# Attention scores from operands stacked on the contraction rows: three matmuls per head and block in place of five

## The chip, the cores and the metric

The kernel runs on one core of one Trainium2 chip. A core has TensorE (PE in the rows; its weight loads are shown as PEld), VectorE (DVE), ScalarE (ACT), GpSimd (POOL) and SyncE (SP, which here only starts DMAs). The metric is device microseconds (us) from start to end of one execution, lower is better. All products are made in an fp32 form (fp32r) with each operand split into a high part, rounded to fp32r, and a low part, the rest; a product is then three matmuls (high by high, low by high, high by low).

## What is computed

Two blocks in a row on 512 tokens of width 1024: the first has attention with a forget gate, a short convolution, a gated merge and a mixture of experts; the second has retention, a Fourier branch and a feed-forward part. The change lies in the attention of the first block alone. Cut to that:

```python
q = rms_norm(q.reshape(b, s, 8, 64), q_norm_g[i])
k = rms_norm(k.reshape(b, s, 8, 64), k_norm_g[i])
log_f = jax.nn.log_sigmoid(f_logit + b_f[i])
...
c = jnp.cumsum(log_f, axis=1).transpose(0, 2, 1)
...
    logits = jnp.einsum('bhqd,bhkd->bhqk', qb, kh) * scale
    logits = logits + (cqb[..., :, None] - c[..., None, :])
    logits = jnp.where(causal, logits, NEG_INF)
    probs = jax.nn.softmax(logits, axis=-1)
    return jnp.einsum('bhqk,bhkd->bhqd', probs, vh)
```

There are 8 heads of 64 features; queries are taken in four blocks of 128, and block qb looks at (qb + 1) * 128 keys.

## The kernel before

The program is one long unrolled list. A scheduler puts each engine's instructions in a fixed order at build time; on the chip each engine runs its list in that order and waits where an operand or a buffer is not there yet. Tiles come from pools by size: `B` tiles (128 x 512 fp32, 35 buffers), `T` tiles (128 x 1024, 5 buffers), and PSUM pools `mm` (4 banks), `sd` (2 banks, for scores and head outputs) and `tp` (2 banks, for transposes; `ptr` takes one).

The stages around the change, in order of time:

- `gemm_q`, `gemm_k`, `gemm_v` project the tokens, one 512-wide block each (`tok_gemm`: 24 matmuls of 512 columns for each weight piece of 256 rows). Each weight piece is cast to its high part `whi` on ACT (L187) and its low part `wlo` is made on DVE (L188). For q and k, `qk_evac` copies each token tile out (`qn`), squares it on ACT, sums on DVE, takes the root on POOL and scales on DVE.
- `forget_gate` is woven into `gemm_k`. It ends with the cumulative sum `csum` (8 heads on 8 partitions), its two parts, and the negated parts. Before the change these go by eight DMAs into four tiles `cq`, `ck`, in which head h owns four partitions: rows (c high, c low, 1, 1) for the queries and (1, 1, -c high, -c low) for the keys.
- `decays` makes 16 exponentials on ACT (`dm_f`, `dm_b`, L647) and three products on DVE (L649, L650) for the second block. It needs two `T` tiles; where it falls in the engines' order is up to the scheduler.
- `qk_turn(hp)` transposes a pair of heads (8 PE transposes into two `tp` banks) and takes them out: one ACT instruction for the high part and one DVE instruction for the low part, for q and for k, each over both heads' 128 partitions. `attention_start` calls it for all four pairs while `gemm_v` runs.
- `attention` runs `values(h)` for the 8 heads, woven with the convolution's projections (`ps_cc`, `ps_cu`, `ps_cb`) and then an output projection (`ps_f`), eight steps of six 512-column matmuls for each head. A head: ten transposes of the probabilities (`pt_p`, from the `tp` banks), `scores(h + 1, (0, 1))`, twelve matmuls with v (`ps_y`), `scores(h + 1, (2, 3))`.
- `scores` makes one block with five matmuls into one `sd` bank: three on the head's 64 rows (L204, L205, L206 inside `mm3`), one on the four gate rows (L851), one bf16 matmul that adds the causal mask on the diagonal (L852). Behind it: maximum on DVE (L854), exponential on ACT (L857), reciprocal and scaling on DVE.

Of the kernel before, what the change touches and what calls it, by code (L numbers as in the profile page):

```python
# [94 lines left out]
def weave(main, side, ratio, drain=True, acc=0.0):  # L95
    """Steps of `main`, with `ratio` steps of `side` traced after each."""
    for _ in main:
        acc += ratio
        while side is not None and acc >= 1.0:
            acc -= 1.0  # L100
            next(side, 0)
        yield 1
    if side is not None and drain:
        yield from side
# [12 lines left out]
class Feed:  # L117
    """Jobs in the order in which their results are used, traced ahead of the use."""
# [4 lines left out]
    def plan(self, jobs):  # L123
        """Queue jobs; the numbers by which to take their results."""
# [15 lines left out]
def fused_blocks(ctx, tc, a, out, probe=None, upto=99):  # L140
# [61 lines left out]
    def mm3(ps, x, y, first, last):  # L202
        """ps (+)= x.T @ y, each operand a (hi, lo) pair."""
# [19 lines left out]
    def tok_gemm(acts, pieces, ktn, evac, nt=NT, last=0, pre=None):  # L223
        """One 512-wide block of acts @ w, tokens on partitions.
        pieces: (offset, width, rows(kt, n)) of the block's columns.
        last: weight pieces at the end that each token tile takes in one go."""
# [41 lines left out]
    def feat_plan(pieces):  # L268
        """[128, 8, 256] of weights as two splits; pieces: (k offset, n, col offset, width, rows)."""
# [11 lines left out]
    def feat_step(nos, acts, name):  # L281
        """The next 128 features of a plan, features on partitions."""
# [5 lines left out]
    def feat4(w, evac, acts):  # L288
        """acts @ w for a w of 512 rows, features on partitions."""
# [27 lines left out]
    def gate_merge(wcols, bias, acts, first, second, dst):  # L317
        """dst = sigmoid(h @ w_a + b_a) * first + sigmoid(h @ w_b + b_b) * second, split."""
# [65 lines left out]
    def sq_sum(x, ss=None):  # L384
        """Sum over the columns given of squares / D."""
# [6 lines left out]
    def first_half(which):  # L392
        """Takes the squares of rows' first halves, for a norm of the whole ones later."""
# [7 lines left out]
    class NormT:  # L401
        """RMS norm of token rows, transposed and split: feature k on partitions."""

        def __init__(self, gain=None, keep=None, over=None, cols=None, on_act=(), on_dve=()):
            """gain: a row on all partitions; or cols: (gain, shift or None) by feature on partitions.
            keep: where the rows go, whose transposes are then kept for the last tile only."""
# [11 lines left out]
        def behind(self, t, x, part, ins, then=None):  # L418
            """do(), with tile t - 1 turned only now, behind ins."""
# [79 lines left out]
    # q, k: per-head norm; v: split  # L499
# [28 lines left out]
    # rows (c, 1) of the queries and (1, -c) of the keys, in high and low parts, c the cumulative  # L528
    # forget gate; head h on partitions 32 (h % 4) + (0 .. 3) of tile h // 4
    cq = [B("cq", F32R), B("cq", F32R)]  # L530
    ck = [B("ck", F32R), B("ck", F32R)]
    for u in cq + ck:
        act.copy(u, bc(one, [P, 512]))
# [11 lines left out]
    # columns of small parameters, by transposing rows of 128  # L545
# [109 lines left out]
    # md rows: shift1, gain1, g1, shift2, gain2, g2, ctx shift, ctx gain  # L655
# [20 lines left out]
    def md_cols(name, gain, shift):  # L676
        """Two of md's rows as columns, features on partitions."""
# [118 lines left out]
    def forget_gate():  # L796
        """Cumulative log sigmoid of the forget gate."""
# [14 lines left out]
        ch, cl, nh, nl = (B("c_" + s, F32R) for s in ("hi", "lo", "nhi", "nlo"))  # L812
        split(csum[:8, :], ch[:8, :], cl[:8, :])
# [92 lines left out]
    def attention():  # L906
        for h in range(8):
            yield from values(h)
# [924 lines left out]
```

## Time and profile before

| | |
|---|---|
| Time, median of three runs | 1509.5 us (1504.53 to 1510.33) |
| The profiled execution: span from first to last instruction | 1516.9 us |
| TensorE busy | 1470.2 us, 97% of the span |
| VectorE, ScalarE busy | 978.6 us, 717.6 us |
| Granted TensorE clock, mean over the span | 0.985 of full speed |
| Chain that ended last, TensorE's share of the span | 51% |

The profiled execution has no time of its own besides its span; the span alone is 7.4 us (0.5%) above the median of the three runs without a profile. A group of instructions is read as: line, engine, operation, output<-inputs, how often, busy time, mean duration. Durations of matmuls overlap, since a matmul starts before the one ahead of it has left the array; what a matmul costs the engine is the distance from its start to the next start.

### The profile page before, as it was taken

To read this page: it belongs to the slowest core of one execution; us is meant where nothing else is said; L and a number is where in the kernel's file an instruction comes from. 1 tells how busy PE (TensorE), PEld (TensorE's weight loads), DVE (VectorE), ACT (ScalarE), POOL (GpSimd) and SP (SyncE) were. 2 spreads that over 40 slices of the span, in tenths; PEclk is the share of its full clock that TensorE was granted. 3 is DMA by queue.
4 is the path that set the end of the run, shared out by engine and by line. 5 is a ranking of instruction groups with operands and counts; after the bars stand their busy time and mean duration, and the time that the engine had idled before them with its cause. 6 is when DMAs were issued, how large, how long until landed. Compare 5 with 4: busy or idle time off the path is not lost.

```text
span 1516.9 us, 18405 instructions
## 1 busy us (share of the span) xinstructions
PE 1470.2 (97%) x6989; PEld 1183.3 (78%) x6989; DVE 978.6 (65%) x1573; ACT 717.6 (47%) x1172; POOL 106.1 (7%) x120
## 2 busy tenths in 40 slices
PE   7999999999999989899999999999999999999997
PEld 5777778887887657677888888888778888888886
DVE  6656464678689988555677777556855664366634
ACT  6643334333459878566444455343345443234432
POOL 2400000000122030311000000000000000000001
PEclk9999999999999999899999999999999999999999
DMA  6421113458489999622322212746623332433221
GB/s 219 123 63 56 56 56 122 159 178 284 149 259 309 369 357 374 217 84 83 105 69 77 67 60 83 238 154 213 218 82 87 108 95 86 112 90 105 80 73 56
DMA packets 174441, 218.99 MB, mean 144 GB/s; under 512 B 9280, under 2 KB 133708, under 8 KB 174348
## 3 DMA queue, kind: packets, MB, share of 16 engines
q1 hardware_dynamic: 169612, 200.98, 40.8%
q0 software_dynamic: 2944, 10.49, 2.2%
q10 hardware_dynamic: 1792, 6.29, 1.1%
q8 instruction: 57, 0.93, 0.3%
q14 instruction: 36, 0.29, 0.1%
HBM read 206.63 MB, written 11.04 MB: 144 GB/s over the span
## 4 chain that ended last, share of the span: by engine, by line
PE 51%; ACT 3%; DVE 2%; issue 1%; POOL 1%; POOLq 0%; ACTq 0%
PE ps_tok L206 6%; PE ps_tok L205 6%; PE ps_tok L204 6%; PE ps_up L204 5%; PE ps_up L205 5%; PE ps_up L206 5%; PE ps_gt L206 2%; PE ps_gt L205 2%; PE ps_gt L204 2%; PE ps_g L204 1%; PE ps_g L206 1%; PE ps_g L205 1%; PE ps_ro L204 1%; PE ps_ro L205 1%; PE ps_ro L206 1%
## 5 line engine op out<-in xcount | busy, mean ns | idle before, releaser
L188 DVE TENSOR_TENSOR wlo<-raw,whi 128x1024 fp32r<-128x1024 f32 x248 | 300.4, 1216 | 265.6 <-ACT whi L187 253.8
L187 ACT CAST whi<-raw 128x1024 fp32r<-128x1024 f32 x248 | 258.1, 1044 | 322.1 <-PE ps_tok L206 119.8
L204 PE MATMUL ps_up<-nt_hi,whi 128*128 128x512 f32 (+2 forms) x368 | 141.5, 385 | 2.8 <-ACT nt_hi L187 2.8
L205 PE MATMUL ps_up<-nt_lo,whi 128*128 128x512 f32 (+2 forms) x368 | 141.6, 385 | 0.0
L206 PE MATMUL ps_up<-nt_hi,wlo 128*128 128x512 f32 (+2 forms) x368 | 141.4, 384 | 0.0
L204 PE MATMUL ps_tok<-whi,nt_hi 128*128 128x512 f32 x288 | 115.3, 402 | 3.2 <-ACT nt_hi L187 3.2
L205 PE MATMUL ps_tok<-wlo,nt_hi 128*128 128x512 f32 x288 | 113.2, 395 | 0.0
L206 PE MATMUL ps_tok<-whi,nt_lo 128*128 128x512 f32 x288 | 112.8, 394 | 0.0
L204 PE MATMUL ps_gt<-nt_hi,whi 128*128 128x512 f32 x256 | 99.7, 389 | 0.0
L205 PE MATMUL ps_gt<-nt_lo,whi 128*128 128x512 f32 x256 | 99.7, 389 | 0.0
L206 PE MATMUL ps_gt<-nt_hi,wlo 128*128 128x512 f32 x256 | 99.7, 389 | 0.0
L204 PEld LDWEIGHTS ps_up<-nt_hi,whi 128*128 128x128 f32 x368 | 69.8, 190 | 16.0 <-ACT nt_hi L187 3.0
L711 DVE SCALAR_TENSOR_TENSOR mod_acc<-raw,silu_c,mod_acc 128x1024 f32<-128x1024 f32 x56 | 70.7, 1277 | 17.0 <-DMA raw<-in_w_mod_dram 16.6
L205 PEld LDWEIGHTS ps_up<-nt_lo,whi 128*128 128x128 f32 x368 | 69.7, 189 | 13.3 <-DVE nt_lo L188 0.2
L206 PEld LDWEIGHTS ps_up<-nt_hi,wlo 128*128 128x128 f32 x368 | 69.7, 189 | 13.1
L188 DVE TENSOR_TENSOR wlo<-raw_a,whi 128x1024 fp32r<-128x1024 f32 x56 | 67.9, 1231 | 3.3 <-ACT whi L187 3.3
L204 PE MATMUL ps_tok<-whi,hid_hi 128*128 128x512 f32 x176 | 68.6, 390 | 0.0
L205 PE MATMUL ps_tok<-wlo,hid_hi 128*128 128x512 f32 x176 | 68.5, 389 | 0.0
L206 PE MATMUL ps_tok<-whi,hid_lo 128*128 128x512 f32 x176 | 68.4, 390 | 0.0
L204 PEld LDWEIGHTS ps_tok<-whi,nt_hi 128*128 128x128 f32 x288 | 54.6, 190 | 15.1 <-ACT nt_hi L187 4.6
L187 ACT CAST whi<-raw_a 128x1024 fp32r<-128x1024 f32 x56 | 58.0, 1051 | 17.8 <-PE ps_tok L206 7.1
L206 PEld LDWEIGHTS ps_tok<-whi,nt_lo 128*128 128x128 f32 x288 | 54.4, 189 | 12.0 <-DVE nt_lo L188 0.9
(461 smaller groups left out, 3334.8 us busy)
## 6 DMA issues: line engine op xcount, KB each, us to landing
raw<-in_w_in_dram SPq DMA_DIRECT2D x31, 1024.0 KB
raw<-in_w_up_dram SPq DMA_DIRECT2D x55, 512.0 KB
raw<-in_w_mod_dram SPq DMA_DIRECT2D x24, 1024.0 KB
raw<-in_w_down_dram SPq DMA_DIRECT2D x15, 1024.0 KB
raw_a<-in_w_gate_dram SPq DMA_DIRECT2D x19, 512.0 KB
raw_a<-in_w_up_dram SPq DMA_DIRECT2D x19, 512.0 KB
raw_a<-in_w_down_dram SPq DMA_DIRECT2D x9, 1024.0 KB
raw<-in_w_branch_gate_dram SPq DMA_DIRECT2D x8, 1024.0 KB
```

Source lines behind the costliest of these rows:

```text
L187: act.copy(hi, src)
L188: return (eng or dve).tensor_tensor(lo, src, hi.bitcast(F32), op=ALU.subtract)
L204: pe.matmul(ps, x[0], y[0], start=first, stop=False)
L205: pe.matmul(ps, x[0], y[1], start=False, stop=False)
L206: pe.matmul(ps, x[1], y[0], start=False, stop=last)
L711: dve.scalar_tensor_tensor(ac, rv[:, j, :], col, ac, op0=ALU.mult, op1=ALU.add)
```

## The change

Each head gets four tiles of its own. `q_hl` holds the high part of q on 64 partitions and its low part on the other 64; `k_hh` holds the high part of k on both halves; `q_hc` holds the high part of q on partitions 0 to 63 and the head's four gate rows on 64 to 67; `k_lc` holds the low part of k and its four gate rows. A block of scores is then one matmul over 128 rows (high by high plus low by high), one over 68 rows (high by low plus the gate term) and the mask matmul as before. The gate rows go from SBUF to a DRAM tile `crows` by four SP DMAs and from there into rows 64 to 67 of each head's tiles by 16 DMAs that POOL issues. `qk_turn` takes a pair out with eight ACT and four DVE instructions of 64 partitions. Turns 0 and 1 stay in `attention_start`; turns 2 and 3 move into `attention`, ahead of `values(2)` and `values(4)`. The rest of the diff takes comments out, which shifts line numbers (the mask matmul L852 becomes L860).

```diff
-    cq = [B("cq", F32R), B("cq", F32R)]
-    ck = [B("ck", F32R), B("ck", F32R)]
-    for u in cq + ck:
-        act.copy(u, bc(one, [P, 512]))
+    crow = [T(n, F32R) for n in ("c_pos", "c_one", "c_neg")]
+    act.copy(crow[1][:8, :], bc(one[:8, :], [8, 1024]))
+    crows = drm.tile([2, 8, 4, S], F32, name="crows")
+    crows_dst = [[crows[0, :, 0:2]], [crows[0, :, 2:4], crows[1, :, 0:2]], [crows[1, :, 2:4]]]
...
-        ch, cl, nh, nl = (B("c_" + s, F32R) for s in ("hi", "lo", "nhi", "nlo"))
-        split(csum[:8, :], ch[:8, :], cl[:8, :])
-        act.mul(nh[:8, :], ch[:8, :].bitcast(F32), -1.0)
-        act.mul(nl[:8, :], cl[:8, :].bitcast(F32), -1.0)
-        for i in range(2):
-            for d, r, s in ((cq, 0, ch), (cq, 1, cl), (ck, 2, nh), (ck, 3, nl)):
-                sp.dma_start(d[i][r:r + 97:32, :].bitcast(F32), s[4 * i:4 * i + 4, :].bitcast(F32))
+        split(csum[:8, :], crow[0][:8, :512], crow[0][:8, 512:])
+        act.mul(crow[2][:8, :], crow[0][:8, :].bitcast(F32), -1.0)
+        for u, dsts in zip(crow, crows_dst):
+            for d in dsts:
+                sp.dma_start(d.rearrange("h i s -> h (i s)"), u[:8, :].bitcast(F32))
...
     def qk_turn(hp):
+        pts = []
         for w in range(2):
             pt = ptr("pt_qk")
             for t in range(NT):
                 pe.transpose(pt[:, t * P:(t + 1) * P], qk[w][t][:, hp * P:(hp + 1) * P], ident)
-            h, l = B("qkT_hi", F32R), B("qkT_lo", F32R)
-            act.activation(h, pt, AF.Copy, scale=gq[:, w:w + 1])
-            dve.scalar_tensor_tensor(l, pt, gq[:, w:w + 1], h.bitcast(F32), op0=ALU.mult, op1=ALU.subtract)
-            qkT[w].append((h, l))
+            pts.append(pt)
+        for j in range(2):
+            h = 2 * hp + j
+            r = slice(64 * j, 64 * j + 64)
+            o = slice(64 - 64 * j, 128 - 64 * j)
+            q, k = pts[0][r, :], pts[1][r, :]
+            g = [gq[r, w:w + 1] for w in range(2)]
+            qs, ks, q2, k2 = (B(n, F32R) for n in ("q_hl", "k_hh", "q_hc", "k_lc"))
+            act.activation(qs[r, :], q, AF.Copy, scale=g[0])
+            act.activation(ks[r, :], k, AF.Copy, scale=g[1])
+            dve.scalar_tensor_tensor(qs[o, :], q, g[0], qs[r, :].bitcast(F32), op0=ALU.mult, op1=ALU.subtract)
+            act.activation(q2[:64, :], q, AF.Copy, scale=g[0])
+            act.activation(ks[o, :], k, AF.Copy, scale=g[1])
+            dve.scalar_tensor_tensor(k2[:64, :], k, g[1], ks[r, :].bitcast(F32), op0=ALU.mult, op1=ALU.subtract)
+            for i, dst in enumerate((q2, k2)):
+                pool.dma_start(dst[64:68, :].bitcast(F32), crows[i, h])
+            head_ops[h] = qs, ks, q2, k2
...
-            mm3(ps[:, :nk], q, k, True, False)
-            pe.matmul(ps[:, :nk], cqh[:, qb * P:nk], ckh[:, :nk], start=False, stop=False)
+            pe.matmul(ps[:, :nk], qs[:, qb * P:nk], ks[:, :nk], start=True, stop=False)
+            pe.matmul(ps[:, :nk], q2[:68, qb * P:nk], k2[:68, :nk], start=False, stop=False)
             pe.matmul(ps[:, qb * P:nk], identb, maskb, start=False, stop=True)
...
     def attention_start():
-        for hp in range(4):
+        for hp in range(2):
             qk_turn(hp)
...
     def attention():
         for h in range(8):
+            if h in (2, 4):
+                qk_turn(h // 2 + 1)
             yield from values(h)
```

On PE, at the scores of a head's blocks 2 and 3 behind twelve projection matmuls, before the change:

```order
L204 MATMUL ps_s<-qkT_hi 128x384
L205 MATMUL ps_s<-qkT_lo,qkT_hi 128x384
L206 MATMUL ps_s<-qkT_hi,qkT_lo 128x384
L851 MATMUL ps_s<-ck,cq 128x384
L852 LDWEIGHTS identb
L852 MATMUL ps_s<-maskb,identb 128x128
L204 MATMUL ps_s<-qkT_hi 128x512
L205 MATMUL ps_s<-qkT_lo,qkT_hi 128x512
L206 MATMUL ps_s<-qkT_hi,qkT_lo 128x512
L851 MATMUL ps_s<-ck,cq 128x512
L852 LDWEIGHTS identb
L852 MATMUL ps_s<-maskb,identb 128x128
```

and in the changed kernel:

```order
L858 MATMUL ps_s<-k_hh,q_hl 128x384
L859 MATMUL ps_s<-k_lc,q_hc 128x384
L860 LDWEIGHTS identb
L860 MATMUL ps_s<-maskb,identb 128x128
L858 MATMUL ps_s<-k_hh,q_hl 128x512
L859 MATMUL ps_s<-k_lc,q_hc 128x512
L860 LDWEIGHTS identb
L860 MATMUL ps_s<-maskb,identb 128x128
```

Four matmuls are gone from each such pair of blocks; nothing else of PE's list moved between them.

On ACT, behind the forget gate, where `c_pos` (before: `c_hi`, `c_lo`) is the cumulative sum and `qn`, `sq` are the k tiles' copies and squares; before the change:

```order
L187 CAST c_hi<-csum 8x512
L187 CAST whi<-raw 128x1024
L814 ACTIVATE c_nhi<-c_hi 8x512
L815 ACTIVATE c_nlo<-c_lo 8x512
L505 COPY qn<-ps_tok 128x512
L506 ACTIVATE sq<-qn 128x512
L505 COPY qn<-ps_tok 128x512
L506 ACTIVATE sq<-qn 128x512
L505 COPY qn<-ps_tok 128x512
L506 ACTIVATE sq<-qn 128x512
L187 CAST whi<-raw 128x1024 x2
```

and in the changed kernel, from the negation on:

```order
L813 ACTIVATE c_neg<-c_pos 8x1024
L647 ACT_TABLE_LOAD
L647 ACTIVATE dm_f<-once,eneg 128x128
L505 COPY qn<-ps_tok 128x512
L647 ACTIVATE dm_f<-once,eneg 128x128
L506 ACTIVATE sq<-qn 128x512
L647 ACTIVATE dm_f<-once,eneg 128x128 x5
L505 COPY qn<-ps_tok 128x512
L647 ACTIVATE dm_f<-once,eneg 128x128
L506 ACTIVATE sq<-qn 128x512
L647 ACTIVATE dm_b<-once,eneg 128x128 x8
L505 COPY qn<-ps_tok 128x512
```

The sixteen exponentials of `decays`, which stood between the q tiles' copies ahead of the forget gate, now stand behind it, with the table load for the exponential ahead of them; on DVE their three products moved in the same way, to behind the forget gate's sum.

On ACT, between the scores of head 2 and the copies of its turned probabilities, before the change:

```order
L857 ACTIVATE pr,rs<-ps_s,nm 128x384
L857 ACTIVATE pr,rs<-ps_s,nm 128x512
L187 CAST whi<-raw 128x1024
L187 CAST p_hi<-pt_p 128x512 x2
L187 CAST p_hi<-pt_p 128x256
```

and in the changed kernel:

```order
L865 ACTIVATE pr,rs<-ps_s,nm 128x384
L865 ACTIVATE pr,rs<-ps_s,nm 128x512
L187 CAST whi<-raw 128x1024
L839 ACTIVATE q_hl<-pt_qk,gq 64x512
L840 ACTIVATE k_hh<-pt_qk,gq 64x512
L843 ACTIVATE k_hh<-pt_qk,gq 64x512
L842 ACTIVATE q_hc<-pt_qk,gq 64x512
L839 ACTIVATE q_hl<-pt_qk,gq 64x512
L840 ACTIVATE k_hh<-pt_qk,gq 64x512
L843 ACTIVATE k_hh<-pt_qk,gq 64x512
L842 ACTIVATE q_hc<-pt_qk,gq 64x512
L187 CAST p_hi<-pt_p 128x512 x2
```

The eight evictions of turn 2 stand there now, ahead of the copies `p_hi`. On PE at the same place the eight transposes of turn 2 are followed by twelve projection matmuls, blocks 0 and 1 of head 3's scores and seven more projection matmuls before the first `pt_p` of head 2, which before stood directly there.

## Rows read from the trace of the kernel before

**Rows 1.** The page, busy time of each engine, and granted clock in 40 slices.

```profile
PE 1470.2 (97%) x6989; PEld 1183.3 (78%) x6989; DVE 978.6 (65%) x1573; ACT 717.6 (47%) x1172; POOL 106.1 (7%) x120
...
PEclk9999999999999999899999999999999999999999
```

**Rows 2.** Windows of 25 us over the attention stage; busy us, then granted clock.

```profile
100.00:125.00 25.00, 25.00 (x122) 18.74 (x121) 12.97 (x29) 10.11 (x24) 0.00 (x0) 1.00 0.28 85
125.00:150.00 25.00, 25.00 (x116) 19.46 (x115) 16.34 (x31) 8.66 (x17) 0.00 (x0) 0.93 0.13 43
150.00:175.00 25.00, 25.00 (x109) 18.34 (x108) 11.68 (x24) 8.17 (x18) 0.00 (x0) 0.93 0.12 43
175.00:200.00 25.00, 25.00 (x109) 19.22 (x108) 13.03 (x27) 8.82 (x19) 0.00 (x0) 0.87 0.13 43
```

**Rows 3.** Timeline of PE, scores of blocks 2 and 3; start, duration.

```profile
171.26 0.39 PE L206 MATMUL ps_cc<-nt_hi,wlo 128*128 128x512 f32 x1
171.58 0.44 PE L204 MATMUL ps_s<-qkT_hi 64*128 64x384 f32 x1
171.86 0.33 PE L205 MATMUL ps_s<-qkT_lo,qkT_hi 64*128 64x384 f32 x1
172.03 0.34 PE L206 MATMUL ps_s<-qkT_hi,qkT_lo 64*128 64x384 f32 x1
172.29 0.43 PE L851 MATMUL ps_s<-ck,cq 4*128 4x384 f32 x1
172.66 0.23 PE L852 MATMUL ps_s<-maskb,identb 128*128 128x128 bf16 x1
172.81 0.50 PE L204 MATMUL ps_s<-qkT_hi 64*128 64x512 f32 x1
173.16 0.39 PE L205 MATMUL ps_s<-qkT_lo,qkT_hi 64*128 64x512 f32 x1
173.39 0.39 PE L206 MATMUL ps_s<-qkT_hi,qkT_lo 64*128 64x512 f32 x1
173.71 0.50 PE L851 MATMUL ps_s<-ck,cq 4*128 4x512 f32 x1
174.14 0.23 PE L852 MATMUL ps_s<-maskb,identb 128*128 128x128 bf16 x1
174.18 0.48 PE L204 MATMUL ps_cc<-nt_hi,whi 128*128 128x512 f32 x1
```

**Rows 4.** Timeline of PE behind that pair of blocks.

```profile
176.34 0.63 PE L204 MATMUL ps_cc<-nt_hi,whi 128*128 128x512 f32 x1
176.77 0.63 PE L205 MATMUL ps_cc<-nt_lo,whi 128*128 128x512 f32 x1
```

**Rows 5.** Timeline of PE, first start of blocks 0 and 1, and the matmul behind them.

```profile
182.60 0.32 PE L204 MATMUL ps_s<-qkT_hi 64*128 64x128 f32 x1
...
184.40 0.48 PE L204 MATMUL ps_cu<-nt_hi,whi 128*128 128x512 f32 x1
```

**Rows 6.** Groups by line, 75 to 242 us; the turn's ACT eviction, a 64-partition one.

```profile
L832 ACT ACTIVATE qkT_hi<-pt_qk,gq 128x512 fp32r<-128x512 f32 x8 | 5.4, 690 | 0.0
...
L187 ACT CAST ya_hi<-ps_y 64x512 fp32r<-64x512 f32 x7 | 4.1, 582 | 6.2 <-PE ps_y L206 6.2
```

**Rows 7.** Timelines of ACT, DVE and PE, 40 to 80 us: exponentials, their product, `wlo`, first use.

```profile
43.28 2.44 ACT L647 ACTIVATE dm_b<-once,eneg 128x128 f32<-128x128 f32 x8
```

```profile
50.77 1.22 DVE L650 TENSOR_TENSOR dm_f<-dm_f,dm_b 128x1024 f32<-128x1024 f32 x1
51.90 0.73 DVE L802 TENSOR_SCALAR z<-ps_f,bf 8x512 f32<-8x512 f32 x1
...
67.80 3.49 DVE L188 TENSOR_TENSOR wlo<-raw,whi 128x1024 fp32r<-128x1024 f32 x3
```

```profile
73.15 0.39 PE L205 MATMUL ps_tok<-wlo,nt_hi 128*128 128x512 f32 x1
```

**Rows 8.** DMA issues by line; the last figure is the median us from issue to landing.

```profile
xg<-h2d,sidx POOLq DMA_INDIRECT x16, 8.3
```

More of the change, by code (lines that the diff above doesn't have):

```diff
@@ L811, in forget_gate @@
         dve.tensor_tensor_scan(csum[:8, :], z[:8, :], zero8[:8, :], 0.0, op0=ALU.add, op1=ALU.add)
-        ch, cl, nh, nl = (B("c_" + s, F32R) for s in ("hi", "lo", "nhi", "nlo"))
-        split(csum[:8, :], ch[:8, :], cl[:8, :])
-        act.mul(nh[:8, :], ch[:8, :].bitcast(F32), -1.0)
-        act.mul(nl[:8, :], cl[:8, :].bitcast(F32), -1.0)
-        for i in range(2):
-            for d, r, s in ((cq, 0, ch), (cq, 1, cl), (ck, 2, nh), (ck, 3, nl)):
-                sp.dma_start(d[i][r:r + 97:32, :].bitcast(F32), s[4 * i:4 * i + 4, :].bitcast(F32))
+        split(csum[:8, :], crow[0][:8, :512], crow[0][:8, 512:])
[3 more added lines that the diff above has]
+                sp.dma_start(d.rearrange("h i s -> h (i s)"), u[:8, :].bitcast(F32))
         yield 1
-    qkT = [[], []]
     interleave(gemm_k, chain(forget_gate(), columns()), R_F)
+    head_ops = {}
     def qk_turn(hp):
+        pts = []
         for w in range(2):
@@ L839, in scores @@
     def scores(h, qbs=range(4)):
-        hp, j = divmod(h, 2)
-        rows = slice(64 * j, 64 * j + 64)
-        base = slice(32 * (h % 4), 32 * (h % 4) + 4)
-        cqh, ckh = cq[h // 4][base, :], ck[h // 4][base, :]
+        qs, ks, q2, k2 = head_ops[h]
         probs.setdefault(h, [])
@@ L847, in scores @@
             ps = psd("ps_s")
-            q = [v[rows, qb * P:nk] for v in qkT[0][hp]]
-            k = [v[rows, :nk] for v in qkT[1][hp]]
-            mm3(ps[:, :nk], q, k, True, False)
-            pe.matmul(ps[:, :nk], cqh[:, qb * P:nk], ckh[:, :nk], start=False, stop=False)
+            pe.matmul(ps[:, :nk], qs[:, qb * P:nk], ks[:, :nk], start=True, stop=False)
+            pe.matmul(ps[:, :nk], q2[:68, qb * P:nk], k2[:68, :nk], start=False, stop=False)
             pe.matmul(ps[:, qb * P:nk], identb, maskb, start=False, stop=True)
```

## The prediction

> **What bounds the kernel now.** The page comes first. TensorE is busy 97% of the span, VectorE 65%, ScalarE 47%, and the granted clock is full in nearly every slice except one near the middle [rows 1]. So a microsecond of TensorE's work counts as a microsecond of the run wherever TensorE does not wait. Windows of the attention stage come second: PE is busy 25.00 of every 25 us there, while DVE and ACT are busy only half or a third of it, and the granted clock falls to 0.93, 0.93 and 0.87 in the three windows from 125 to 200 us, though it is 1.00 before [rows 2]. The slices of the page hide this dip, because a slice is 38 us long. What is to be seen: TensorE's own instructions set the pace here, and part of the time they run at the lower clock.
>
> The timeline of PE is third. In the projection stream a 512-column matmul follows the one ahead by 0.23 us. The pair of score blocks 2 and 3 takes from 171.58 to 174.18, 2.60 us for ten matmuls [rows 3]; blocks 0 and 1 take from 182.60 to 184.40, 1.80 us [rows 5]. A head's scores hold 5632 columns (four matmuls of 1280 columns together and 512 for the mask), which at 0.23 us for 512 would be 2.53 us of the 4.40. So 1.87 us per head are not columns: they sit at the changes between operands of 64 rows, of 4 rows and the bf16 mask. L206 to L851 takes 0.32 us with 512 columns, L851 to L852 takes 0.43, L204 to L205 takes 0.35 [rows 3].
>
> The dip last. Behind that same pair of blocks the projection matmuls follow one another at 0.43 us, not 0.23, about half the speed: this is the lower of the two clock levels, 1.2 GHz in place of 2.4 [rows 3, 4]. Right before it fell the engine had not waited: it ran the pair of blocks with 64 and 4 rows. The three windows lose 25 x (0.07 + 0.07 + 0.13) = 6.75 us of full-speed work [rows 2].
>
> **The change, part by part.** *Two matmuls fewer for each block.* In blocks 2 and 3, L205 takes 0.17 and 0.23 us to the next start and L206 takes 0.26 and 0.32, together 0.98 of 2.60 us [rows 3]. The same share, 38%, of the 1.80 us of blocks 0 and 1 [rows 5] is 0.68. That is 1.66 us per head, 13.3 us for eight heads. From below, only their columns go: 2560 columns per head at 0.23 us for 512 are 1.15 us, 9.2 us in all.
>
> *Fewer changes of operand shape.* The stream pays 0.32 in place of 0.23 us when it enters the blocks (171.26 to 171.58) [rows 3]; with operands of 128 rows on both sides I expect this gone: 16 entries x 0.09 = 1.4 us. L851 takes 0.43 us where 512 columns take 0.23 [rows 3]. Its place is taken by a matmul of 68 rows ahead of the same mask. If the extra 0.20 us belongs to the four rows it goes, if it belongs to the mask it stays; no row parts the two. Between 0 and 32 x 0.20 = 6.4 us I take the half, 3.2. The 0.12 us extra of L204 behind the mask (0.35 against 0.23, 3.8 us in all) I leave in, since the mask stands there as before; from above it goes too. Together this part gives 13.3 + 1.4 + 3.2 = 17.9 us, with ends of 9.2 (columns alone) and 13.3 + 1.4 + 6.4 + 3.8 = 24.9.
>
> A rule of the Trainium skill speaks against it. The page "TensorE: Matmul & The Clock Gate", section "Part 3: Packing small matmuls — row/col tiling", says that a weight load overlaps a running matmul only when the two use different row groups; stacking on all rows takes that chance away. By it each of the 64 stacked matmuls would show its load, and with 0.12 us for one (L204's extra) this part would give 17.9 - 7.7 = 10.2 us. The trace has as many loads as matmuls [rows 1], and matmuls of 128 rows behind one another at 0.23 us, with no load to be seen between them [rows 3], so I go by the row and not by the rule.
>
> *The clock.* The low stretch comes only behind the pairs of 64- and 4-row blocks. With 128 and 68 rows and about 1.2 us less of them in the pair, I expect no fall: 6.75 us come back. From below, nothing does.
>
> *Evictions of the turns.* Before, a turn cost ACT two instructions of 0.69 us; a 64-partition one takes 0.58 us [rows 6], so eight take 4.7 us, and the two `tp` banks are held until the last of them. Turns 0 and 1: the second turn's transposes wait for the first one's evictions, with some twenty projection matmuls (4.6 us) between them in PE's list. Turns 2 and 3: before `pt_p` PE's list has nineteen projection matmuls (4.4 us) and two blocks of scores (about 1.1 us by the sum above), 5.5 us of cover for 4.7 us of ACT and one DVE instruction behind it. What is late next when the cover fails is `p_hi`, and with it `ps_y`. ACT has the time in sum: 9 of 25 us busy [rows 2]. I take 0.75 us of wait for each of four turns, 3 us; the ends are nothing and 10 us (half of each eviction burst shows).
>
> *The gate rows' way through DRAM.* Sixteen POOL DMAs, on a queue with nothing behind them until the experts. What waits for them is L859, and all of PE behind it. The nearest row is POOL's indirect DMA with 8.3 us from issue to landing [rows 8]. For heads 2 to 7 the lead is longer than that: blocks 2, 3 and the next blocks 0, 1 alone lie 11.0 us apart [rows 3, 5]. For head 0 POOL is free once the last root of `gemm_k` is done, shortly ahead of the turn. I take 0, with 4 us once as the other end. The four SP DMAs in place of eight wait for the same engines and stand ahead of weights that are not needed for tens of us: 0.
>
> *What the scheduler moved.* The sixteen exponentials (eight take 2.44 us, so 4.9) and a table load now stand on ACT ahead of the second weight piece of `gemm_v`, and three products of 1.22 us on DVE ahead of its `wlo`. Before, that `wlo` began at 67.80 (three take 3.49, so the first is done at 69.0) and PE needed it at 73.15: 4.1 us of cover [rows 7]. The added ACT work is 4.9 us plus about 1.3 for the load; against it the forget gate's chain starts earlier, because `z` at 51.90 stood behind those same three products (the last at 50.77) [rows 7]; some 2 us of 3.7 come back there, since other small DVE work of `decays` moves in between. So 4.2 us later against 4.1 us of cover, and the products on DVE partly beside ACT: I take 1 us, with ends of 0 and 4. The exponentials' table load was paid before at head 0's softmax, so it is only moved.
>
> **The sum.** 17.9 + 6.75 - 3 - 0 - 1 = 20.65 us against the span of 1516.9 us: 1496.2. The span stands 7.4 us above the median of the runs shown, 1509.5, so the time becomes 1509.5 - 20.65, about 1489 us. A gain here stays, since what follows is started by PE's progress and the buffers that it frees.
>
> **The rivals.** *The clock still falls.* For it: it falls elsewhere too, [rows 1] has a weak slice behind 600 us, where there are no scores, and what decides is not known from the rows; a changed rhythm may only move the fall. Then 20.65 - 6.75 = 13.9 us are gained: 1495.6.
> *The turns make PE wait.* For it: both `tp` banks are held for 4.7 us, and the cover is nearly the same length. Against it: ACT and DVE have time. With 10 us in place of 3 and the prologue at 4: 10.65 gained, 1498.9.
> *Weight loads show:* each stacked matmul, on the same rows as the one ahead of it, pays L204's extra 0.12 us [rows 3], 64 x 0.12 = 7.7 us; 12.95 us are gained, 1496.5. Against it stand the 0.23 us of the stream. This is what the Trainium skill states on the page named above.
> *Slower:* the gate rows land late and PE stands at L859. With its place at each head's first block, it decides from 20.65 us over eight heads, 2.6 us per head. A lateness of 4 us in each head gives 8 x 4 - 20.65 = 11.35 us more, 1521. Against it speaks the lead of 11 us, above 8.3, for all heads but the first two.
> *No change:* the extra stays at the mask and at the entries (9.2 us), the clock falls all the same, and 7 us are lost to waits: 2 us gained, 1507.
>
> **Numbers.** Half a per cent, 7.5 us, is about what a measurement of this kernel can tell from no change; the three runs span 5.8 us. My forecast has 0.55; the clock still falling 0.17; the turns' waits 0.10; the loads 0.05; no change 0.07; slower 0.06. The predicted time is 1489 us. The forecast's own range is 1480 to 1495: at its lower end the blocks give all but 2 us of their upper bound of 24.9 (7 us more than the sum), at its upper end 6 us less. Taking in the first three rivals, which lie at 1495.6 to 1498.9, with 2 us for a mixture of them, gives 1480 to 1501; what is left out is no change, slower, and the ends of the forecast. Faster by over 0.5%: 0.55 + 0.17 + 0.10 + 0.05 = 0.87; within: 0.07; slower: 0.06.
>
> **What would show it.** Right: blocks 2 and 3 take about 1.5 us from first to next start, blocks 0 and 1 about 1.0; the granted clock is 1.00 in all windows from 100 to 225 us; a head is about 2.2 us shorter at full clock; PE shows no wait above 1 us behind a turn. Wrong: 0.3 us or more from L858 to L859 at 128 columns (loads show), PE idle ahead of L859 until a DMA, PE idle ahead of `pt_p` or the second `pt_qk` until an eviction, PE idle at 72 to 75 us until `wlo`, or a clock below 1 behind score blocks.

## The result and the profile after

The changed kernel takes 1485.95 us (median of four runs, 1485.43 to 1486.66) against 1509.91 us (median of four, 1504.53 to 1514.04): a ratio of 0.9843, with a 95% interval of 0.9814 to 0.9873. That is 24.0 us less; 1489.0 us was forecast. Its profiled execution took 1485.43 us with a span of 1483.5 us.

The page, with the lines that answer to [rows 1]:

```profile
PE 1437.3 (97%) x6925; PEld 1166.1 (79%) x6925; DVE 981.3 (66%) x1581; ACT 731.5 (49%) x1192; POOL 112.1 (8%) x136
...
PEclk9999999999999999999999999999999999999999
```

TensorE has 64 matmuls and 32.9 us of busy time less, and is still the engine that sets the pace. The windows of the attention stage, columns as in [rows 2]:

```profile
125.00:150.00 25.00, 24.68 (x133) 19.82 (x132) 19.00 (x38) 15.06 (x30) 0.00 (x0) 1.00 0.15 45
150.00:175.00 25.00, 24.69 (x131) 20.27 (x129) 16.45 (x33) 15.51 (x33) 2.08 (x4) 1.00 0.24 83
```

The granted clock is 1.00 here, ScalarE has gone from 8 or 9 us to 15 of 25, and TensorE waits 0.3 us in each of these two windows. The timeline of PE at blocks 2 and 3, which answers to [rows 3]:

```profile
157.17 0.39 PE L206 MATMUL ps_cc<-nt_hi,wlo 128*128 128x512 f32 x1
157.40 0.33 PE L858 MATMUL ps_s<-k_hh,q_hl 128*128 128x384 f32 x1
157.57 0.33 PE L859 MATMUL ps_s<-k_lc,q_hc 68*128 68x384 f32 x1
157.75 0.23 PE L860 MATMUL ps_s<-maskb,identb 128*128 128x128 bf16 x1
157.79 0.48 PE L858 MATMUL ps_s<-k_hh,q_hl 128*128 128x512 f32 x1
158.10 0.40 PE L859 MATMUL ps_s<-k_lc,q_hc 68*128 68x512 f32 x1
158.34 0.23 PE L860 MATMUL ps_s<-maskb,identb 128*128 128x128 bf16 x1
158.38 0.47 PE L204 MATMUL ps_cc<-nt_hi,whi 128*128 128x512 f32 x1
```

From 157.40 to 158.38 the pair takes 0.98 us, in place of the 2.60 of [rows 3]; 1.5 was forecast. Blocks 0 and 1 of the same kind take 0.58 us (164.84 to 165.42), in place of the 1.80 of [rows 5]. The mask matmul, which started 0.37 us behind L851 before, now follows 0.18 us behind a 384-column matmul: nothing but that matmul's columns is left ahead of it. Behind the mask an extra stays: the 512-column L858 takes 0.31 us to the next start, 0.08 more than the stream's 0.23. The waits of PE from 25 to 260 us, with total, count and longest:

```profile
PE pt_p L884 <- ACT q_hc L842: 1.5, 3, 0.9
PE ps_cc L204 <- DVE v_lo L188: 0.2, 1, 0.2
```

Three short waits at `pt_p` behind turns and one for a low part of v; none for a gate row's DMA, none for `wlo`.

One difference between the two profiles comes first: the spans differ by 33.4 us, the medians by 24.0.

### The profile page after: what moved, and what is told of

The parts are those of the page before. It is cut to its first block, busy times and chain, and to the rows that moved or that the text cites. A ratio compares the mean times of both kernels' runs of the same rounds, so it can differ in the third digit from the quotient of the medians.

```text
span 1483.5 us, 18370 instructions
## 1 busy us (share of the span) xinstructions
PE 1437.3 (97%) x6925; PEld 1166.1 (79%) x6925; DVE 981.3 (66%) x1581; ACT 731.5 (49%) x1192; POOL 112.1 (8%) x136
## 4 chain that ended last, share of the span: by engine, by line
PE 52%; ACT 3%; DVE 2%; issue 2%; POOL 1%; POOLq 0%; ACTq 0%
PE ps_tok L206 6%; PE ps_tok L204 6%; PE ps_tok L205 6%; PE ps_up L204 6%; PE ps_up L205 5%; PE ps_up L206 5%; PE ps_gt L205 2%; PE ps_gt L206 2%; PE ps_gt L204 2%; PE ps_g L204 1%; PE ps_g L206 1%; PE ps_g L205 1%; PE ps_ro L204 1%; PE ps_ro L205 1%; PE ps_ro L206 1%
## 5 line engine op out<-in xcount | busy, mean ns | idle before, releaser
L204 PE MATMUL ps_up<-nt_hi,whi 128*128 128x512 f32 (+2 forms) x368 | 141.4, 385 | 2.8 <-ACT nt_hi L187 2.8
L204 PE MATMUL ps_tok<-whi,nt_hi 128*128 128x512 f32 x288 | 115.0, 402 | 1.0 <-ACT nt_hi L187 1.0
L204 PE MATMUL ps_gt<-nt_hi,whi 128*128 128x512 f32 x256 | 99.6, 389 | 0.0
L204 PEld LDWEIGHTS ps_up<-nt_hi,whi 128*128 128x128 f32 x368 | 69.7, 190 | 16.0 <-ACT nt_hi L187 3.0
L204 PE MATMUL ps_tok<-whi,hid_hi 128*128 128x512 f32 x176 | 68.5, 389 | 0.0
L204 PEld LDWEIGHTS ps_tok<-whi,nt_hi 128*128 128x128 f32 x288 | 55.1, 191 | 12.7 <-ACT nt_hi L187 2.0
```

The source lines that it names most:

```text
L204: pe.matmul(ps, x[0], y[0], start=first, stop=False)
```

## The experiments

**e1: the kernel before, once more.**

> The kernel before, unchanged, profiled once more. Question: of the 33.4 us between the two profiled spans, 6.6 us lie behind the attention, in the expert stage, though the medians differ by only 24.0 us. Theory A (those 6.6 us are a difference between executions, in waits on ScalarE and VectorE, not the change's): a second profile of the kernel before has its last expert matmul and the second block's first transpose several us earlier than 604.5 and 744.2 us, and a span of 1503 to 1512 us. Rival (they come from the change): the landmarks stand at 604 and 744 us again, within 1 us. Both: the granted clock falls in attention again, to 0.85 to 0.95 in windows of 25 us; were it 1.00 there, the fall would be a matter of the execution and not of the kernel.

It took 1507.13 us, span 1505.4. The first and last start of the experts' first matmul, in this run and then in the changed kernel (duration min, median, max in ns, then the two starts):

```profile
L204 PE MATMUL ps_gu<-whi,xgT_hi x128: 389/393/722, 446.4 to 597.6; 128*96 128x512 f32 x128
```

```profile
L204 PE MATMUL ps_gu<-whi,xgT_hi x128: 389/393/722, 421.3 to 573.2; 128*96 128x512 f32 x128
```

From first to last it is 151.2 us here and 151.9 in the changed kernel; in the first profile of the kernel before it was 156.5 (448.0 to 604.5). The second block's first transpose starts at 734.9 us in place of 744.2. So theory A holds: the excess in the expert stage belongs to that one execution, and the change's gain lies ahead of that stage, which starts 25.1 us earlier in the changed kernel than here. The granted clock fell in the attention again, in two windows up to 225 us and once more in the next:

```profile
150.00:175.00 25.00, 25.00 (x110) 18.49 (x109) 12.16 (x26) 8.95 (x20) 0.00 (x0) 0.93 0.12 43
...
200.00:225.00 25.00, 25.00 (x111) 19.14 (x111) 13.22 (x29) 10.10 (x22) 0.00 (x0) 0.93 0.18 59
```

That is 3.5 us up to 225 us, where [rows 2] has 6.75: how often it falls differs from one execution to the next.

**e2: the stacking alone undone.**

```diff
-            pe.matmul(ps[:, :nk], qs[:, qb * P:nk], ks[:, :nk], start=True, stop=False)
-            pe.matmul(ps[:, :nk], q2[:68, qb * P:nk], k2[:68, :nk], start=False, stop=False)
+            pe.matmul(ps[:, :nk], q2[:64, qb * P:nk], ks[:64, :nk], start=True, stop=False)
+            pe.matmul(ps[:, :nk], q2[:64, qb * P:nk], k2[:64, :nk], start=False, stop=False)
+            pe.matmul(ps[:, :nk], qs[:64, qb * P:nk], ks[:64, :nk], start=False, stop=False)
+            pe.matmul(ps[:, :nk], q2[64:68, qb * P:nk], k2[64:68, :nk], start=False, stop=False)
```

(In even heads the high and low parts of q change halves in `q_hl`, so that all products lie on rows 0 to 63.)

> The changed kernel with the stacking alone undone: three matmuls of 64 rows, one of 4 gate rows and the mask from the new tiles; the evictions, the gate rows' way, the turns' places and the scheduler's list otherwise as in the changed kernel, nothing of the computation left out. Theory A (most of the gain is in changes of operand shape on top of the columns, and the clock falls behind thin-row blocks): the pair of blocks 2 and 3 takes 2.6 us again, blocks 0 and 1 take 1.8, some 24 us over eight heads, the clock falls in attention again for 7 us: 1510 to 1518 us, at or above the kernel before. Rival B (columns alone count): 64 matmuls with 1.15 us of columns per head, 9.2 us: 1495 us at a full clock. Rival C (the gain comes from the reordered list, not from the matmuls): within 3 us of 1486.

1509.83 us (1507.24 to 1513.41), ratio 0.9995 (0.9975 to 1.0014). The blocks are as long as in [rows 3, 5] (2.60 and 1.79 us) and PE's waits behind the turns are gone; that the longer blocks cover them is likely, not shown. So the matmuls account for the whole gain, 23.9 us by the medians, and evictions, gate rows and moved turns together cost nothing that the medians can tell. The traces put it a little lower. `ps_gt`, the first matmul behind the attention, starts at 271.3 us in e1, 268.3 here and 246.3 in the changed kernel: 22.0 us go with the matmuls and 3.0 with the rest, in which e1's falls of the clock are contained. Columns alone (rival B) and the reordered list (rival C) are out. One half of theory A fell: with these thin blocks the clock did not fall:

```profile
150.00:175.00 25.00, 25.00 (x118) 18.37 (x117) 13.51 (x28) 9.47 (x22) 2.08 (x4) 1.00 0.13 44
175.00:200.00 25.00, 25.00 (x128) 18.84 (x126) 18.72 (x34) 13.97 (x27) 0.00 (x0) 1.00 0.19 65
```

**e3: the gate rows by themselves.**

```diff
-            pe.matmul(ps[:, :nk], q2[:68, qb * P:nk], k2[:68, :nk], start=False, stop=False)
+            pe.matmul(ps[:, :nk], q2[:64, qb * P:nk], k2[:64, :nk], start=False, stop=False)
+            pe.matmul(ps[:, :nk], q2[64:68, qb * P:nk], k2[64:68, :nk], start=False, stop=False)
```

> The changed kernel with the gate rows taken out of the second matmul: a stacked one of 128 rows, one of 64 rows, one of 4 rows and the mask; nothing of the computation left out. It adds 1280 columns per head, 0.58 us, 4.6 us in all. Theory A1 (the four rows cost their entry, 0.2 us each time, as L851's 0.43 for 0.23): 32 x 0.2 = 6.4 us more and some entries of the 64-row matmul, 1497 us (1494 to 1501). Theory A2 (the extra belongs to the mask behind them): the columns alone, 1490.6 us. If the clock falls again in attention, up to 7 us on top of either; theory A has it fall less than with five matmuls.

1502.74 us (1500.49 to 1505.58), ratio 0.9962 (0.9948 to 0.9975): 16.8 us for 4.6 us of columns, more than either reading gave. PE's timeline of blocks 2 and 3:

```profile
167.03 0.33 PE L858 MATMUL ps_s<-k_hh,q_hl 128*128 128x384 f32 x1
167.29 0.43 PE L859 MATMUL ps_s<-k_lc,q_hc 64*128 64x384 f32 x1
167.66 0.44 PE L860 MATMUL ps_s<-k_lc,q_hc 4*128 4x384 f32 x1
168.03 0.23 PE L861 MATMUL ps_s<-maskb,identb 128*128 128x128 bf16 x1
168.07 0.48 PE L858 MATMUL ps_s<-k_hh,q_hl 128*128 128x512 f32 x1
```

A 384-column matmul is worth 0.17 us. Into the 64-row one it takes 0.26, into the 4-row one 0.37, into the mask 0.37: an extra at each place where the number of rows goes from one class to another (128, 64, 4, 128). The mask takes no extra of its own ahead of it; the 0.08 us behind it is apart from these, since the changed kernel has it too.

**e4: the same columns as before, no thin rows.**

```diff
             pe.matmul(ps[:, :nk], qs[:, qb * P:nk], ks[:, :nk], start=True, stop=False)
+            pe.matmul(ps[:, :nk], qs[:, qb * P:nk], ks[:, :nk], start=False, stop=False)
             pe.matmul(ps[:, :nk], q2[:68, qb * P:nk], k2[:68, :nk], start=False, stop=False)
+            pe.matmul(ps[:, :nk], q2[:68, qb * P:nk], k2[:68, :nk], start=False, stop=False)
```

> The changed kernel with each of its two score matmuls issued twice, so five matmuls per block with the columns of the kernel before, but of 128, 128, 68, 68 rows and the mask; the scores are therefore twice what they should be. Theory A (a thin operand and a change of shape cost the excess, and thin rows bring the clock down): only the columns come back, 2560 per head, 1.15 us, 9.2 us: 1495 us (1493 to 1498), the pair of blocks 2 and 3 takes 1.8 us, clock 1.00 in attention. Rival (number of matmuls, each with its load): 64 x 0.12 = 7.7 us more, 1503. Rival on the clock (a rhythm of the head's length brings it down, not the rows): granted clock below 0.95 in some windows from 100 to 225 us, some 7 us more.

1494.92 us (1492.52 to 1499.10), ratio 0.9911 (0.9888 to 0.9934); the clock stays at 1.00, and the pair takes 1.80 us (162.23 to 164.03):

```profile
162.23 0.33 PE L858 MATMUL ps_s<-k_hh,q_hl 128*128 128x384 f32 x1
...
162.98 0.47 PE L858 MATMUL ps_s<-k_hh,q_hl 128*128 128x512 f32 x1
163.29 0.39 PE L859 MATMUL ps_s<-k_hh,q_hl 128*128 128x512 f32 x1
163.51 0.40 PE L860 MATMUL ps_s<-k_lc,q_hc 68*128 68x512 f32 x1
163.75 0.40 PE L861 MATMUL ps_s<-k_lc,q_hc 68*128 68x512 f32 x1
163.99 0.23 PE L862 MATMUL ps_s<-maskb,identb 128*128 128x128 bf16 x1
164.03 0.48 PE L204 MATMUL ps_cc<-nt_hi,whi 128*128 128x512 f32 x1
```

Five matmuls cost 9.0 us more than three, which is their columns (9.2), and 14.9 us less than five thin ones with the same columns. More matmuls as such, with a load each, cost nothing beyond their columns.

**e5 and e6: same matmuls and columns as the changed kernel, the second one on 64 rows, or on 4.**

```diff
-            pe.matmul(ps[:, :nk], q2[:68, qb * P:nk], k2[:68, :nk], start=False, stop=False)
+            pe.matmul(ps[:, :nk], q2[:64, qb * P:nk], k2[:64, :nk], start=False, stop=False)
```

```diff
-            pe.matmul(ps[:, :nk], q2[:68, qb * P:nk], k2[:68, :nk], start=False, stop=False)
+            pe.matmul(ps[:, :nk], q2[64:68, qb * P:nk], k2[64:68, :nk], start=False, stop=False)
```

> The changed kernel with its second score matmul on 64 rows in place of 68, and nothing else: the gate term is left out of the scores. The same number of matmuls and the same columns as the changed kernel; what differs is that 64 rows fit half of the array's rows, where 68 do not, so the array's row mode changes twice per block (into the 64-row matmul and out of it). Theory D (each change of row mode, from above 64 rows to 64 or to 32 and fewer and back, costs about 0.17 us: e3 has three per block and 0.50 us per block above its columns): 32 x 2 x 0.17 = 10.9 us, 1493 to 1497 us, the pair of blocks 2 and 3 takes 1.65 us in place of 0.98. Rival F (the four-row matmul alone is dear): 1485 to 1488 us, pair still 0.98.

> The changed kernel with its second score matmul on the four gate rows alone: the product of high by low is left out of the scores. Matmuls and columns as in the changed kernel. Theory D (a change of row mode costs, whatever the mode): like the 64-row form, 1493 to 1497 us and 1.65 us for the pair of blocks 2 and 3. Rival F (the four-row matmul alone is dear, 0.2 us before and 0.2 us behind it): 32 x 0.4 = 12.8, 1497 to 1500, while the 64-row form is at 1486. Third reading (a change costs by how far the row mode goes, 128 to 32 more than 128 to 64): this one slower than the 64-row form by 3 us or more.

1493.60 us (1490.25 to 1494.49), ratio 0.9909 (0.9894 to 0.9924), and 1492.73 us (1490.57 to 1494.36), ratio 0.9905 (0.9890 to 0.9920). Taking four rows away from a matmul costs some 7 us. PE's timeline in the 64-row form:

```profile
161.00 0.33 PE L858 MATMUL ps_s<-k_hh,q_hl 128*128 128x384 f32 x1
161.26 0.43 PE L859 MATMUL ps_s<-k_lc,q_hc 64*128 64x384 f32 x1
161.63 0.23 PE L860 MATMUL ps_s<-maskb,identb 128*128 128x128 bf16 x1
161.66 0.47 PE L858 MATMUL ps_s<-k_hh,q_hl 128*128 128x512 f32 x1
162.07 0.50 PE L859 MATMUL ps_s<-k_lc,q_hc 64*128 64x512 f32 x1
162.50 0.23 PE L860 MATMUL ps_s<-maskb,identb 128*128 128x128 bf16 x1
162.54 0.48 PE L204 MATMUL ps_cc<-nt_hi,whi 128*128 128x512 f32 x1
```

Line by line this is the timeline of the changed kernel above, with 64 for 68: 1.54 us in place of 0.98, 0.56 us for four changes, 0.14 each (0.17 was expected). In the 4-row form the same pair takes 1.54 us too. So theory D holds, at a lower price than it named, and neither four rows (rival F) nor the distance between the classes matters.

**e7: the five thin matmuls, two blocks at a time.**

```diff
+                pair = [(b, (b + 1) * P, psd("ps_s")) for b in (qb, qb + 1)]
+                for i, (x, y) in enumerate(((q2[:64], ks[:64]), (q2[:64], k2[:64]), (qs[:64], ks[:64]), (q2[64:68], k2[64:68]))):
+                    for b, nk, ps in pair:
+                        pe.matmul(ps[:, :nk], x[:, b * P:nk], y[:, :nk], start=i == 0, stop=False)
+                for b, nk, ps in pair:
+                    pe.matmul(ps[:, b * P:nk], identb, maskb, start=False, stop=True)
```

> The five-matmul form from the new tiles (64, 64, 64 and 4 rows and the mask), issued for two blocks together: each kind of operand for both blocks, then the next kind. Nothing is left out; the same matmuls and columns as with five matmuls block by block (1509.8 us), but three changes of row mode per pair of blocks in place of six. Theory D: 16 pairs x 0.5 us = 8 us less, 1500 to 1504 us, the pair of blocks 2 and 3 takes 2.1 us in place of 2.6. Rival G (each thin matmul pays, wherever it stands): 1508 to 1512 us, pair at 2.6. Against both: the first block of a pair is complete only with the second, so VectorE's maximum starts later; if that shows, PE waits at the score banks or ahead of the transposes of the probabilities.

1502.45 us (1499.56 to 1508.15), ratio 0.9963 (0.9946 to 0.9981), 7.4 us less than e2 with the same matmuls in another order. (The kernel before took 1507.22 us beside this one and 1508.81 beside e2; by the first start of `ps_gt`, 263.1 against 268.3, the difference is 5.2.) The pair takes 2.10 us, 166.48 to 168.58:

```profile
166.48 0.66 PE L861 MATMUL ps_s<-k_hh,q_hc 64*128 64x384 f32 x2
166.99 0.57 PE L861 MATMUL ps_s<-k_lc,q_hc 64*128 64x384 f32 x2
167.39 0.57 PE L861 MATMUL ps_s<-k_hh,q_hl 64*128 64x384 f32 x2
167.89 0.66 PE L861 MATMUL ps_s<-k_lc,q_hc 4*128 4x384 f32 x2
168.49 0.28 PE L863 MATMUL ps_s<-maskb,identb 128*128 128x128 bf16 x2
168.58 0.48 PE L204 MATMUL ps_cc<-nt_hi,whi 128*128 128x512 f32 x1
```

That is three changes fewer for 0.50 us, and 0.30 above e4's 1.80 for the three that are left. The rival is out. In this order neighbouring matmuls also write to two banks in turn; e5 and e6 keep the order of the banks and show the price without that. No new wait of more than 0.2 us appeared.

**e8: q out of the transposes first.**

```diff
+        for (r, o), (qs, _, q2, _) in zip(rows, ops):
+            q = pts[0][r, :]
...
+        for (r, o), (_, ks, _, k2) in zip(rows, ops):
+            k = pts[1][r, :]
```

> The changed kernel with a turn's evictions in another order: all of q for both heads, then all of k, so that the transpose bank of q comes free after four ScalarE instructions in place of seven; nothing left out. The changed kernel has three PE waits at the transposes of the probabilities behind the turns, 1.5 us in all. If the held bank is their cause, they go: 1484 to 1485 us. Rival (the probabilities wait for ScalarE's work as a whole, whichever bank is free): the waits stay, 1486 us or more, since the high parts of k now come later for scores.

1487.14 us (1485.60 to 1488.61), ratio 0.9873 (0.9857 to 0.9888). A miss, on the side of the rival: PE's waits there come to 2.1 us in all, 1.4 of it still at `pt_p` behind the turn's evictions on ScalarE. The held bank was not the cause, or not alone.

**e9: turns moved in the kernel before.**

```diff
-        for hp in range(4):
+        for hp in range(2):
             qk_turn(hp)
...
         for h in range(8):
+            if h in (2, 4):
+                qk_turn(h // 2 + 1)
```

> The kernel before with turns 2 and 3 moved into the attention, as in the change, and nothing else; nothing left out. Its score blocks are those of the kernel before, five matmuls with three row-mode changes. Question: the clock, which fell in the attention in both profiles of the kernel before and in none of the kernels with the new evictions, thin blocks or not. Theory H (the fall goes with the transposes and evictions standing together ahead of the attention, not with the blocks): granted clock 1.00 in all windows from 100 to 225 us, mean clock 0.992 or more, 1504 to 1508 us. Rival I (it goes with the blocks and the head's length, and five_thin escaped by accident): the clock falls again in one to four windows, 1507 to 1512 us. Either way the move by itself costs no more than 1 us of waits, since a turn here has two ScalarE instructions of 0.69 us.

1508.45 us (1506.41 to 1513.95), ratio 1.0016 (1.0004 to 1.0027): the move by itself gains nothing. The clock was 1.00 in four windows up to 200 us and fell in the last (and in the next one, to 250):

```profile
175.00:200.00 25.00, 25.00 (x123) 18.75 (x122) 17.38 (x36) 9.56 (x22) 0.00 (x0) 1.00 0.25 85
200.00:225.00 25.00, 25.00 (x114) 19.28 (x113) 13.30 (x26) 10.05 (x20) 0.00 (x0) 0.93 0.14 43
```

Theory H falls. The run is as rival I has it, but in all the clock fell in the attention in the three profiles with the old evictions and in none of the eleven others, five of which have thin rows (e2, e3, e5, e6, e7), so that the blocks alone are not it either. They mark the place: each of the nine falls in those three profiles begins within 1 us behind blocks 2 and 3 of a head (in e1 behind the pairs that end at 152.27, 210.30 and 231.06 us), but most such pairs bring none. What brings it down there stays open; a kernel with the old matmuls' tiles and the new evictions' load was not tried.

**e10: the mask on VectorE.**

```diff
-            pe.matmul(ps[:, :nk], q2[:68, qb * P:nk], k2[:68, :nk], start=False, stop=False)
-            pe.matmul(ps[:, qb * P:nk], identb, maskb, start=False, stop=True)
+            pe.matmul(ps[:, :nk], q2[:68, qb * P:nk], k2[:68, :nk], start=False, stop=True)
+            dve.tensor_tensor(ps[:, qb * P:nk], ps[:, qb * P:nk], maskb, op=ALU.add)
```

> The changed kernel with the causal mask added by VectorE in the score bank (128 columns per block) in place of the third matmul; nothing left out. Theory D (behind the stacking only columns and the bf16 mask's own entry are left): the mask's 4096 columns are 1.84 us, the 0.09 us of extra behind it 16 times 1.4, the rest of the blocks' excess over their columns (0.06 and 0.12 us per pair) 1.4 us: 4.6 us less, 1481 to 1483 us. Rival J (the maximum now waits for one more VectorE instruction, some 0.3 us for each of 32 blocks; banks and probabilities come later): PE waits at the transposes of the probabilities or at the score banks take it back, 1485 to 1488 us.

1482.10 us (1481.26 to 1484.00), ratio 0.9835 (0.9820 to 0.9851). The pair of blocks 2 and 3 takes 0.81 us, the stream behind it goes on at 0.24 in place of 0.32, and the 32 additions take 293 ns each on VectorE, which had room. The wait at the transposes stays at 1.4 us. The ratio's interval overlaps that of the changed kernel, whose times were not taken beside these; e11, whose edit moves one instruction of the changed kernel, was timed beside them and took 1484.81. The first start of `ps_gt` is at 243.2 us in place of 246.3. So this version is ahead of the changed kernel by some 3 us by the trace and the times of e11, and 25 ahead of the kernel before.

**e11: the row of ones made later.**

```diff
-    act.copy(crow[1][:8, :], bc(one[:8, :], [8, 1024]))
...
         split(csum[:8, :], crow[0][:8, :512], crow[0][:8, 512:])
+        act.copy(crow[1][:8, :], bc(one[:8, :], [8, 1024]))
```

> The changed kernel with the cast of the row of ones issued behind the split of the cumulative gate in place of the program's start; nothing left out. In the changed kernel that cast is ScalarE's first instruction, the scheduler puts the first low part of a weight ahead of the first normed tile on VectorE, and PE's first tile transposes start at 10.2 us in place of 8.6, from where everything runs about 1 us later. Theory K (that order is the cause): the first transposes start at 8.6 to 9.0 us, the landmarks to the end come 1 us earlier, 1484.5 to 1485.5 us. Rival (the first weights' transfers set it): start at 10 us again, 1486 us.

1484.81 us (1483.66 to 1487.31), ratio 0.9852 (0.9834 to 0.9871). The first tile transposes start earlier, but the first projection matmul does not; PE's timeline here and then in the changed kernel, where a wait for the low part of the first tile follows:

```profile
8.79 2.15 PE L453 MATMUL pt_n<-misc,xn 128*128 128x128 f32 x8 [0.67 <-DVE xn L439]
13.36 0.80 PE L204 MATMUL ps_tok<-whi,nt_hi 128*128 128x512 f32 x1 [2.42 <-ACT nt_hi L187]
```

```profile
10.16 1.97 PE L453 MATMUL pt_n<-misc,xn 128*128 128x128 f32 x8 [2.21 <-DVE xn L439]
13.14 0.79 PE L204 MATMUL ps_tok<-whi,nt_hi 128*128 128x512 f32 x1 [1.01 <-ACT nt_hi L187]
...
15.26 0.80 PE L206 MATMUL ps_tok<-whi,nt_lo 128*128 128x512 f32 x1 [0.90 <-DVE nt_lo L188]
```

The wait of 0.90 us is gone here, as it is in e1, so that the second tile's transposes start at 15.52 us in place of 16.29. But of this only 0.3 us is left at the fourth tile's (26.69 against 26.98; 25.87 in e1) and at the first `ps_gt` (246.0 against 246.3). The time lies in theory K's range and its interval takes in the rival's 1486. So theory K is right about the transposes, and the 1 us that was to follow did not come.

**e12: the mask on VectorE, second copies on POOL.**

```diff
-            act.activation(q2[:64, :], q, AF.Copy, scale=g[0])
+            pool.tensor_copy(q2[:64, :], qs[r, :].bitcast(F32))
-            act.activation(ks[o, :], k, AF.Copy, scale=g[1])
+            pool.tensor_copy(ks[o, :], ks[r, :].bitcast(F32))
```

> The mask on VectorE, and besides it the second copies of a turn's high parts (four per turn, from SBUF to the other 64 partitions) made by POOL in place of ScalarE, so that ScalarE has four instructions per turn, 2.35 us, in place of eight, and the transpose banks come free when ScalarE's four and VectorE's four are done; nothing left out. With the mask on VectorE alone the run took 1482.1 us, and PE waited 1.4 us in all at the transposes of the probabilities behind three turns. Theory L (those waits are ScalarE's time for a turn): they go, 1480 to 1481.5 us. Rival M (POOL's copies are slow, 1 to 2 us each by its tensor instruction of 128x256 at 1.17 us, and the scores of a turn's first head need them): PE waits at the score matmuls behind POOL for some us in each of four turns, 1484 to 1490 us.

1484.05 us (1481.83 to 1488.46), ratio 0.9833 (0.9808 to 0.9859), no different from e10. PE's waits from 25 to 260 us:

```profile
PE ps_s L859 <- DMA k_lc<-crows: 1.7, 1, 1.7
PE pt_p L884 <- DVE q_hl L841: 1.1, 3, 0.5
```

ScalarE's half of a turn is off the list, VectorE's takes its place, and the gate rows, queued on POOL behind its copies, come late once. Theory L falls; the wait that M names comes once in place of four times.

## Why the prediction was right

The main step, that matmuls and changes of shape go and their time with them, is right. That the time lies only 3 us from the forecast is in part luck. By the medians the blocks gave 6.0 us more than their term, and all the rest together 0.1 in place of 2.75 (6.75 of the clock less 4 for turns and scheduler): the misses go in opposite directions.

*Two matmuls fewer, and fewer changes of shape.* Forecast 17.9 us with ends of 9.2 and 24.9; e2 measures 23.9. Adding up the distances from each score matmul to the next start, without the waits among them (0.9 us after, 0.8 in e4), gives 35.7 us in the kernel before (both profiles), 13.3 after and 23.5 in e4: 10.2 us go with the columns (9.2 as worked out), the other 12.2 (and the 0.09 us at entries) with changes of rows. The term was mis-sized at "Between 0 and 32 x 0.20 = 6.4 us I take the half, 3.2" and at leaving L204's extra behind the mask in. Both put an extra at a matmul. It sits at the change between two row classes. With the thin rows gone, the whole extra of 0.20 us went from ahead of the mask (0.43 to 0.24 us), and from the mask's start to the start of the second matmul behind it 0.50 us [rows 3] became 0.35, with 0.08 of extra left; so the sum landed near the upper bound. By the medians, less the columns, a change costs 0.13 us in e3 (96 changes), 0.12 and 0.11 in e5 and e6 (64 each) and 0.15 in e7 (48): one price within the spread of the runs.

A rule of the Trainium skill says this: the page "TensorEngine Tiling (Array Packing)", section "Tiling Modes", states that changing the tiling mode, and not just the tile, drains TensorE. The traces agree in that each change costs 0.13 to 0.17 us, with 68 rows counting as 128; that it is a drain no trace here shows.

*The clock.* Forecast 6.75 us back. The changed kernel's attention does run at 1.00, but the size of the fall in [rows 2] belonged to that one execution: in e1 it is 3.5 us up to 225 us. Over the whole span nothing came back against e1: with mean clocks of 0.992 and 0.991, e1 loses about 12 us to the low clock and the changed kernel about 13, none of it in the attention; the first profile of the kernel before, at 0.985, lost 23. Over 65 runs of the kernel before the mean granted clock is 0.991 in the median (0.982 to 0.995); the four runs of the changed one have 0.990 to 0.993. The step that failed is the reason given, that "the low stretch comes only behind the pairs of 64- and 4-row blocks": in the attention the falls do begin there, but e2, e3, e5, e6 and e7 have such blocks at a full clock. Taking the fall from one profile, whose span stood 7.4 us above the median, as a property of the kernel over-sized the term.

*The turns.* Forecast 3 us (0 to 10): 1.5 us of waits, at `pt_p`, where the prediction looked for them. What holds them is not settled: e8 speaks against the held bank alone, e12 against ScalarE's work alone.

*The gate rows' way.* Forecast 0: no wait at L859. e12, where POOL is late with one, shows what it costs: 1.7 us once.

*What the scheduler moved.* Forecast 1 us at `wlo`: no wait there. PE does run 0.9 us later than in e1 when the turns begin (first `pt_qk` at 79.4 against 78.5 us). It starts with the wait of 0.90 us at 15.26 us, which e1 does not have; taking it away, as e11 does, brought back only 0.3, and why is open.

*The sum.* From the span's start to the first `ps_gt`, e1 takes 271.3 us and the changed kernel 246.3, 25.0 less. The terms: 22.4 us from the score matmuls' distances, 1.4 at the entries, 5.2 of the clock (three stretches of some 1.7 in e1 up to 236 us), less 1.7 of waits and 0.9 of the later start: 26.4, 1.4 more than measured, which is not traced. Behind it e1 takes 1234.1 us, the changed kernel 1237.2 and the first profile of the kernel before 1244.1 (1516.9 - 272.8): the two executions of one kernel lie further apart than the two kernels.

*The rivals.* Loads do not show: L858 to L859 takes 0.17 us for 384 columns, and e4's 64 more matmuls cost only columns. The rule of the Trainium skill weighed there, on the page "TensorE: Matmul & The Clock Gate", section "Part 3: Packing small matmuls — row/col tiling", asks for different row groups if a load is to overlap; the same rows were used here, and the load was hidden all the same. (The prediction cites [rows 3] for matmuls of 128 rows at 0.23 us; the pair at that distance there has 64 rows. e4's lines show it with 128 and 68 rows, 163.29 to 163.75, at 0.22 and 0.24.) Late gate rows and long turns did not come. The clock did not fall in the attention; over the whole span it fell as much as in e1.

## What to carry to other kernels

Where matmuls with few contraction rows stand between full ones, count the changes between row classes, not only matmuls and columns: fill the rows (68 in place of 64 was worth 7 us here), or group blocks of one class. Put an extra that a timeline shows at a transition and ask on which side it goes; a variant with equal columns settles it. Take what varies between executions, as the clock's falls do, from several of them before it enters a sum.

## What the runs showed of the hardware

A change between 128 or 68 rows, 64 rows and 4 rows cost 0.13 to 0.17 us of TensorE's time by differences between pairs of blocks (0.80 us for six changes between e2 and e4, 0.56 for four in e5 and e6, 0.50 for three between e2 and e7), the same from 128 to 64 and back as from 128 to 4 and back (1.54 us for the pair in both). Behind the bf16 mask matmul the next fp32 one took 0.08 us more than its columns, with 128 rows on both sides; without the mask, in e10, this extra is gone. The load for a matmul of 68 rows behind one of 128 on the same rows did not show (0.17 us for 384 columns). Falls of the granted clock in the attention came in three of three profiles with the old evictions and in none of the eleven others, at places and in numbers that differ between executions of one kernel.
